# Moving two of four LRU column tiles into the S5 column pass, with twelve token places and a lighter GpSimd

## Chip, cores and metric

One core of a Trainium2 chip runs the whole program. The metric is the device time of one execution in microseconds (us), lower is better.

## What is computed

The reference is one transformer-like layer: a hybrid mixer and then a SwiGLU FFN, both with normalised, modulated input. What matters here is the mixer's front half:

```
h_lat = rms_norm(x, g) * (1 + sc1) + sh1          # 2048 tokens x 1024
h_ctx = rms_norm(ctx, g) * (1 + csc1) + csh1      # 256 tokens
u, xr, gr = split(h @ w_in)                       # 512 S5, 512 LRU, 512 gate columns
y_s5 = s5_scan(u) ...                             # complex diagonal states, both directions
y_lru = rglru(conv(xr)) * gelu(gr_lat)            # gate columns for latent tokens alone
out = concat(y_s5, y_lru) @ w_out
```

All of it is float32. A matrix product is made of three float32r products (high by high, high by low, low by high).

## The kernel before

**The work.** The tokens go through in five groups: n = 0 is the 256 context tokens, n = 1 to 4 are 512 latent tokens each. The 1536 columns of `w_in` are twelve column tiles of 128: four S5 tiles, four LRU tiles, four gate tiles. One product, of one group and one column tile, is 8 x 3 matmuls into a PSUM tile `pu`. The context group needs no gate columns.

**Stages.** `front` (line 159) runs three generators beside each other. `vectors` makes the modulation. `s5_prep` makes the S5 parameters and, through `s5_tables`, sixteen rotation tables (`tb`, stored in TAB), the matrices PKE and PKC and, last, MD from `kx`. `u_pass` makes the four S5 tiles of all five groups: for each group it loads the tokens (`xt`), scales them by their norm (line 352), and `turn` transposes them (`pt`), modulates (`y`), splits them into high and low (`ht`), and stores `y` in HD for groups 0 to 3. Two sets of eight `ht` tiles serve alternate groups, so the next group's turning may begin while the current group's products still run. Its results go to UD.

`mix` (line 183) then runs `s5_main`: 16 channel pairs in two directions, 32 states. A state is four small products `pv` on PE, then some ten instructions on VectorE (lines 753 to 770) with two scans, and the outputs `py` are products again. As filling work between them, `rest_pass` (line 807) makes the LRU and gate tiles: group 4 first, whose `ht` tiles are still in place, then groups 0 to 3, whose tokens come back from HD (`hty`) and are split again (`ht<-hty`). It has fourteen places for these. `AHEAD` says how many of its 36 products are written ahead of the first state, and `S5_FILL` how much filling a state is owed.

**The order.** Inside `s5_main` the PE order is the written one. Everywhere else a scheduler at build time sets each engine's order, and every engine then works through its instructions in that order.

**A table's steps** (`s5_tables`, lines 697 to 709): on GpSimd two scalings of a ramp (`tbf`), a rounding in two steps (`tbw`) and a subtraction; on VectorE two corrections (line 702); on ScalarE sines; on VectorE a product (line 707); on ScalarE the last two steps.

Of the kernel before, what the change touches and what calls it, by code (L numbers as in the profile page):

```python
# [9 lines left out]
F32 = mybir.dt.float32  # L10
# [35 lines left out]
class Hybrid:  # L46
# [102 lines left out]

    AHEAD = 8  # L150
    S5_FILL, CONV_FILL, DECAY_FILL, GATES_FILL = 4.2, 0.1, 2.0, (0, 2, 2, 2)
    VW = 5
# [5 lines left out]
    def front(self):  # L158

        self.ies, self.ues = ExitStack(), ExitStack()  # L160
        self.wip = self.pool(self.ies, "winp", 1)

        self.htp = self.pool(self.ies, "htp", 1)
# [138 lines left out]
    def load_w_in(self, col0, pool, stage, place=None):  # L302

        ws = []
        src = self.A["w_in"][0].rearrange("(k p) f -> p k f", p=128)
        for m in range(4):
            c0 = col0 + m * 128
            if place:
                wh, wl = (t.rearrange("p a (b f) -> p (a b) f", f=128) for t in place[m])
            else:  # L310
                wh, wl = (pool.tile([128, KT, 128], F32R, name=f"win{nm}{m}") for nm in "hl")
            raw = stage()
            self.nc.sync.dma_start(raw, src[:, :, c0:c0 + 128])
            self.split(wh, wl, raw)
            ws.append((wh, wl))
        return ws

    def ht(self, n, k):
        return self.htp.tile([128, 2, 512], F32R, name=f"ht{n % 2}_{k}")

    def u_pass(self, es):

        nc, A = self.nc, self.A
        sp = self.pool(es, "us", 2)
        lent = iter(range(KT))
        whole = lambda: self.ht(1, next(lent)).bitcast(F32).rearrange("p a f -> p (a f)")

        def load(n):
            if n == 0:
                xt = [whole() for _ in range(2)]  # L330
# [13 lines left out]
        def norm(tiles, junk):  # L344
# [29 lines left out]
        def product(n, m, hts, after):  # L374
# [7 lines left out]
            ut = sp.tile([128, 512], F32, name="ut")  # L382
            if n == 0:
                uv = ut[:, :CTX].rearrange("p (t j) -> p t j", t=T)
# [8 lines left out]

        ws0 = [whole().rearrange("p (k f) -> p k f", k=KT) for _ in range(4)]
        xs = load(0)
        norm(xs, whole())
        yield
        ws = self.load_w_in(0, self.wip, ws0.pop)
        yield
# [4 lines left out]
        hts = []  # L404
        turn(0, xs, hts, range(KT))
        raw = lambda: xp.tile([128, D], F32, name="xt").rearrange("p (k f) -> p k f", k=KT)
        for n in range(5):
# [10 lines left out]
            for m in range(4):  # L418
                if (n, m) == (4, 2):

                    place = [(self.ht(1, i), self.ht(1, i + 4)) for i in range(4)]
                    self.wrest = self.load_w_in(512, None, raw, place=place)
                product(n, m, hts, after)
                yield 5.2
# [261 lines left out]
    def s5_tables(self, p, st, fh, fl):  # L686
# [6 lines left out]
        for k in range(NPAIR):  # L693
            f = st.tile([128, 2, NPOS], F32, name="tbf")
            w = st.tile([128, 2, NPOS], F32, name="tbw")
            for d in range(2):
                nc.gpsimd.tensor_scalar(f[:, d], jr, fh[:, d * 16 + k:d * 16 + k + 1], 0.0, op0=MUL, op1=ADD)
            nc.gpsimd.tensor_scalar(w, f, 1.0, MAGIC, op0=MUL, op1=ADD)
            nc.gpsimd.tensor_scalar(w, w, 1.0, -MAGIC, op0=MUL, op1=ADD)
            nc.gpsimd.tensor_tensor(f, f, w, op=SUB)  # L700
            for d in range(2):
                v.scalar_tensor_tensor(f[:, d], jr, fl[:, d * 16 + k:d * 16 + k + 1], f[:, d], op0=MUL, op1=ADD)
            tb = st.tile([128, 2, 2, NPOS], F32, name="tb")
# [104 lines left out]
    def rest_pass(self, es):  # L808

        nc = self.nc  # L810
        st = self.pool(es, "ist", 2)
        hp = self.pool(es, "gtp", 1)
# [15 lines left out]
        for n, after in ((4, 0), (0, 1), (1, 2), (2, 3), (3, None)):  # L828
# [6 lines left out]

            for m in range(8 if n else 4):
                more(min(MORE, m + 1 if n else 2 * m + 2))
                pu = ps.tile([128, 512], F32, name="pu")
                wh, wl = self.wrest[m]
# [3 lines left out]
                ut = st.tile([128, 512], F32, name="iev")  # L843
                if m >= 4:
                    nc.scalar.activation(ut, pu, AF.Gelu_apprx_tanh)
                    nc.sync.dma_start(self.GGD[m - 4][:, (n - 1) * 512:n * 512], ut)
                elif n == 0:
                    nc.scalar.activation(ut[:, :CTX].rearrange("p (j t) -> p t j", t=T),
                                         pu[:, :CTX].rearrange("p (t j) -> p t j", t=T), AF.Copy)
                    nc.sync.dma_start(self.XRD[m][:, 0:CTX], ut[:, :CTX])  # L850
                else:

                    for t in range(2):
                        nc.scalar.activation(ut.rearrange("p (c t r) -> p t r c", c=8, t=2)[:, t],
                                             pu.rearrange("p (t r c) -> p t r c", t=2, c=8)[:, t], AF.Copy)
                    dst = self.XRD[m][:, CTX:CTX + SEQ].rearrange("p (c x) -> p c x", c=8)
                    nc.sync.dma_start(dst[:, :, (n - 1) * 64:n * 64], ut.rearrange("p (c x) -> p c x", c=8))
                yield 5.4 if n else 2.8
# [721 lines left out]
```

## Time and profile before

| | |
|---|---|
| Median of 3 runs | 2353.78 us (2349.54 to 2354.25) |
| The profiled execution: own time | 2348.0 us |
| Its span, first to last instruction | 2346.2 us |
| Busy: PE, VectorE, ScalarE, GpSimd | 2105.7, 1714.1, 966.3, 905.5 us |
| Mean granted TensorE clock | 0.947 |

The span is what the profile's rows cover; 1.8 us of the execution's own time lie around it. PE is busy for 90% of the span, but as an average over stages: the first 240 us and the stage of the states differ much from the FFN behind them, so the stages are read apart. In the rows DVE is VectorE, ACT is ScalarE, POOL is GpSimd, SP is the engine that issues most DMAs, PEclk the granted share of full clock.

### The profile page before, as it was taken

What the parts mean: (1) busy time and instruction counts of PE and PEld (TensorE: products, weight loads), DVE (VectorE), ACT (ScalarE), POOL (GpSimd) and SP (SyncE); (2) the same over time, 40 slices, a digit from 0 to 9 for tenths busy, and PEclk for the clock granted to TensorE, in tenths of its full rate; (3) what the DMA queues carried; (4) which work ended last, traced back from release to release, by engine and by line L of the source; (5) the groups of instructions that cost most, each with busy time, mean ns of one, the idle gap of its engine ahead of it and who ended that gap; (6) DMA issues with size and microseconds to landing.
All of it is one profiled execution on the core that took longest, in us unless ns stands there. A gap on an engine that the chain in (4) does not pass through costs nothing. (4 is left out here: it accounts for less than half of the span.)

```text
span 2346.2 us, 27426 instructions
## 1 busy us (share of the span) xinstructions
PE 2105.7 (90%) x9460; PEld 1664.3 (71%) x9460; DVE 1714.1 (73%) x2227; ACT 966.3 (41%) x1511; POOL 905.5 (39%) x560
## 2 busy tenths in 40 slices
PE   6578999899475699869999999999999999999997
PEld 1466776667374578747888888788888878888885
DVE  6987338997898766866778887987777763534669
ACT  2566421211766734773333333433333333232433
POOL 4786240340000002342334553666665620400674
PEclk8689999999788899979999999999999999999999
DMA  8476866664334366883444333544444374734673
GB/s 246 154 219 232 257 208 180 208 195 128 118 110 145 109 202 211 273 259 122 135 143 135 108 99 127 171 161 148 152 152 155 137 255 158 229 105 143 205 268 115
DMA packets 311626, 403.28 MB, mean 172 GB/s; under 512 B 60176, under 2 KB 222528, under 8 KB 309952
## 3 DMA queue, kind: packets, MB, share of 16 engines
q1 hardware_dynamic: 311360, 401.50, 52.8%
q8 instruction: 75, 1.23, 0.2%
q14 instruction: 63, 0.52, 0.1%
q0 software_dynamic: 128, 0.04, 0.0%
HBM read 269.33 MB, written 132.12 MB: 171 GB/s over the span
## 5 line engine op out<-in xcount | busy, mean ns | idle before, releaser
L70 PE MATMUL fp<-op,fws 128*128 128x512 f32 x1232 | 485.0, 394 | 7.8 <-ACT op L59 7.1
L71 PE MATMUL fp<-op,fws 128*128 128x512 f32 x1232 | 485.1, 394 | 5.3 <-DVE op L62 3.1
L72 PE MATMUL fp<-op,fws 128*128 128x512 f32 x1232 | 484.0, 393 | 0.0
L70 PEld LDWEIGHTS fp<-op,fws 128*128 128x128 f32 x1232 | 232.6, 189 | 62.1 <-ACT op L59 9.2
L71 PEld LDWEIGHTS fp<-op,fws 128*128 128x128 f32 x1232 | 232.2, 188 | 60.5 <-DVE op L62 5.4
L72 PEld LDWEIGHTS fp<-op,fws 128*128 128x128 f32 x1232 | 232.2, 189 | 51.5
L1337 POOL TENSOR_TENSOR fs<-fraw 128x512 f32<-128x512 f32 x44 | 65.8, 1495 | 490.8 <-DMA fraw<-in_w_ffn_in_dram 408.4
L1017 PE MATMUL po<-gw,ga 128*128 128x512 f32 x616 | 240.7, 392 | 4.3 <-ACT ga L59 2.9
L1018 PE MATMUL po<-gw,ga 128*128 128x512 f32 x616 | 240.5, 392 | 0.9 <-DVE gw L62 0.9
L1019 PE MATMUL po<-gw,ga 128*128 128x512 f32 x616 | 237.8, 391 | 2.4 <-DVE ga L62 2.4
L62 DVE TENSOR_TENSOR fws<-fraw,fws 128x512 fp32r<-128x512 f32 x132 | 128.8, 977 | 58.2 <-ACT fws L59 57.3
L59 ACT ACTIVATE fws<-fraw 128x512 fp32r<-128x512 f32 x132 | 82.8, 629 | 142.6 <-PE fp L72 76.0
L1017 PEld LDWEIGHTS po<-gw,ga 128*128 128x128 f32 x616 | 116.6, 189 | 29.7 <-ACT ga L59 3.8
L1019 PEld LDWEIGHTS po<-gw,ga 128*128 128x128 f32 x616 | 116.0, 188 | 27.8 <-DVE ga L62 3.9
L1018 PEld LDWEIGHTS po<-gw,ga 128*128 128x128 f32 x616 | 116.5, 189 | 26.2 <-DVE gw L62 1.7
L62 DVE TENSOR_TENSOR ga<-gys,ga 128x1024 fp32r<-128x1024 f32 (+2 forms) x88 | 119.2, 1358 | 13.3 <-ACT ga L59 13.0
L71 PE MATMUL pu<-ht,winh 128*128 128x512 f32 (+1 forms) x288 | 115.1, 400 | 14.5 <-DVE ht L62 14.5
L62 DVE TENSOR_TENSOR fws<-fs,fws 128x512 fp32r<-128x512 f32 x132 | 118.2, 896 | 9.7 <-ACT fws L59 8.0
L59 ACT ACTIVATE fws<-fs 128x512 fp32r<-128x512 f32 x132 | 82.4, 625 | 94.3 <-PE fp L72 92.5
L70 PE MATMUL pu<-ht,winh 128*128 128x512 f32 (+1 forms) x288 | 114.2, 405 | 3.7 <-ACT ut L390 3.2
L72 PE MATMUL pu<-ht,winl 128*128 128x512 f32 (+1 forms) x288 | 113.2, 393 | 0.0
L62 DVE TENSOR_TENSOR gw<-graw,gw 128x512 fp32r<-128x512 f32 x44 | 37.8, 860 | 84.0 <-ACT gw L59 83.9
(509 smaller groups left out, 4733.8 us busy)
## 6 DMA issues: line engine op xcount, KB each, us to landing
fraw<-in_w_ffn_in_dram SPq DMA_DIRECT2D x88, 512.0 KB, 4.4
graw<-in_w_ffn_out_dram SPq DMA_DIRECT2D x99, 256.0 KB, 3.9
gys<-S SPq DMA_DIRECT2D x44, 512.0 KB, 3.8
A<-faf SPq DMA_DIRECT2D x33, 512.0 KB, 2.6
S<-ost SPq DMA_DIRECT2D x33, 512.0 KB, 3.1
alw<-in_w_ada_dram SPq DMA_DIRECT2D x24, 512.0 KB, 5.1
ost<-A SPq DMA_DIRECT2D x22, 512.0 KB, 4.3
gys<-A SPq DMA_DIRECT2D x22, 512.0 KB, 5.1
```

Of the source, the lines that this page charges most:

```text
L59: self.nc.scalar.activation(hi, src, AF.Identity)
L62: (eng or self.nc.vector).tensor_tensor(lo, src, hi.bitcast(F32), op=SUB)
L70: mm(ps, wh, xh, start=first, stop=False)
L71: mm(ps, wh, xl, start=False, stop=False)
L72: mm(ps, wl, xh, start=False, stop=last)
L1017: mm(ps, xh, wh, start=first, stop=False)
L1018: mm(ps, xh, wl, start=False, stop=False)
L1019: mm(ps, xl, wh, start=False, stop=last)
L1337: g.tensor_tensor(s[0], a21, a22, op=ADD)
```

## The change

It does four things.

- `u_pass` makes six column tiles for each group: the four S5 tiles and LRU tiles 0 and 1 (`end_rest` stores these). The weights of the two are kept in four new tiles `wx`. `rest_pass` makes the other two LRU tiles and the four gate tiles: 26 products instead of 36. `AHEAD` goes from 8 to 2, `S5_FILL` from 4.2 to 3.9.
- The `ht` tiles are one ring of twelve places instead of two sets of eight. Tiles 4 to 7 of the next group take the places of tiles 0 to 3 of the current one, so they are turned within the last product (steps 40 to 43 of 48), tiles 0 to 3 at steps 22 to 34. `rest_pass` has twelve places instead of fourteen: four `wx` and the eight of group 4.
- A table's two ramp scalings go from GpSimd to ScalarE; the second half of the rounding and the subtraction become one VectorE instruction of 128x576.
- The scaling of the tokens goes from GpSimd to ScalarE.

```diff
-    AHEAD = 8
-    S5_FILL, CONV_FILL, DECAY_FILL, GATES_FILL = 4.2, 0.1, 2.0, (0, 2, 2, 2)
+    AHEAD = 2
+    S5_FILL, CONV_FILL, DECAY_FILL, GATES_FILL = 3.9, 0.1, 2.0, (0, 2, 2, 2)
...
-    def ht(self, n, k):
-        return self.htp.tile([128, 2, 512], F32R, name=f"ht{n % 2}_{k}")
+    HT = 12
+
+    def ht(self, i):
+        return self.htp.tile([128, 2, 512], F32R, name=f"ht{i % self.HT}")
+
+    def wx(self, i):
+        return self.wxp.tile([128, 2, 512], F32R, name=f"wx{i}")
...
-                nc.gpsimd.tensor_scalar(x, x, rs[:, i:i + 1], 0.0, op0=MUL, op1=ADD)
+                nc.scalar.activation(x, x, AF.Copy, scale=rs[:, i:i + 1])
...
-                ht = self.ht(n, k)
+                ht = self.ht(8 * n + k)
...
+            if m >= 4:
+                self.end_rest(n, m - 4, pu, ut)
...
+        ws += self.load_w_in(512, None, lambda: next(stages), [(self.wx(2 * i), self.wx(2 * i + 1)) for i in range(2)])
...
-                if nxt and i % 2 and len(nh) < KT and i >= 13:
+                if nxt and i in (22, 26, 30, 34, 40, 41, 42, 43):
                     turn(n + 1, nxt, nh, (len(nh),))
...
-            for m in range(4):
+            for m in range(6):
...
-                nc.gpsimd.tensor_scalar(f[:, d], jr, fh[:, d * 16 + k:d * 16 + k + 1], 0.0, op0=MUL, op1=ADD)
+                nc.scalar.activation(f[:, d], jr, AF.Copy, scale=fh[:, d * 16 + k:d * 16 + k + 1])
             nc.gpsimd.tensor_scalar(w, f, 1.0, MAGIC, op0=MUL, op1=ADD)
-            nc.gpsimd.tensor_scalar(w, w, 1.0, -MAGIC, op0=MUL, op1=ADD)
-            nc.gpsimd.tensor_tensor(f, f, w, op=SUB)
+            v.scalar_tensor_tensor(f, w, -MAGIC, f, op0=ADD, op1=SUB)
...
-        MORE = 6
-        places = cycle([lambda i=i: hp.tile([128, 2, 512], F32R, name=f"ht{i}") for i in range(MORE)] +
-                       [lambda k=k: self.ht(0, k) for k in range(KT)])
+        MORE = 4
+        places = cycle([lambda i=i: self.wx(i) for i in range(MORE)] + [lambda i=i: self.ht(i) for i in range(32, 40)])
...
-            for m in range(8 if n else 4):
+            for i in range(6 if n else 2):
```

**The instruction order at the first state, on PE.** Before, the last eight products ahead of the first `pv` are all of `rest_pass`, for group 4 (gate weights `winh`, `winl`); behind it stand context products of 256 columns (operands `ht`, weights in `ht` places):

```order
L70 MATMUL pu<-ht_7_2174,winh_2494 128x512
L71 MATMUL pu<-ht_7_2174,winh_2494 128x512
L72 MATMUL pu<-ht_7_2174,winl_2495 128x512
L747 MATMUL pv<-u,pe 64x288 x4
L70 MATMUL pu<-ht_2517,ht_0_2369 128x256
L71 MATMUL pu<-ht_2517,ht_0_2369 128x256
L72 MATMUL pu<-ht_2517,ht_4_2370 128x256
```

With the change the first row of `pv` stands two products ahead of the end of `u_pass` (its last S5 product ahead of it, weights `winh`, then its two LRU products, weights `wx`):

```order
L70 MATMUL pu<-ht_2548,winh_475 128x512
L71 MATMUL pu<-ht_2548,winh_475 128x512
L72 MATMUL pu<-ht_2548,winl_476 128x512
L774 MATMUL pv<-u,pe 64x288
L70 MATMUL pu<-ht_2402,wx_565 128x512
L71 MATMUL pu<-ht_2402,wx_565 128x512
L72 MATMUL pu<-ht_2402,wx_566 128x512
```

The first state's last `pv` rows stand behind 720 `pu` matmuls (30 products, six of the context) instead of 672 (28, four of the context), the second state's behind 792 instead of 720. The last product of `s5_prep` (`pk`) stands behind 456 `pu` matmuls instead of 336. In both orders the last `pv` row has 1320 to 1344 of all 1344 `pu` matmuls ahead of it.

**On VectorE at the same place.** Before, splits of tokens read back (`hty`) stand ahead of the first state and inside it:

```order
L62 TENSOR_TENSOR ht_2_2860<-hty,ht_2_2860 128x512
L62 TENSOR_TENSOR ht_3_2865<-hty,ht_3_2865 128x512
L62 TENSOR_TENSOR ht_4_2898<-hty,ht_4_2898 128x512
L753 TENSOR_TENSOR ta<-pv,tab 128x576
L754 TENSOR_TENSOR tb__2812<-pv,tab 128x576
L62 TENSOR_TENSOR ht_5_2903<-hty,ht_5_2903 128x512
L62 TENSOR_TENSOR ht_6_2961<-hty,ht_6_2961 128x512
L62 TENSOR_TENSOR ht_7_2966<-hty,ht_7_2966 128x512
L755 TENSOR_TENSOR ta<-ta,tb__2812 128x288
```

With the change weight splits (`winl`) stand ahead of it and the first token splits behind its last row:

```order
L62 TENSOR_TENSOR winl_2764<-xt,winh_2763 128x1024
L62 TENSOR_TENSOR winl_2770<-xt,winh_2769 128x1024
L780 TENSOR_TENSOR ta<-pv,tab 128x576
L781 TENSOR_TENSOR tb__2894<-pv,tab 128x576
L782 TENSOR_TENSOR ta<-ta,tb__2894 128x288
L783 TENSOR_TENSOR ta<-ta,tb__2894 128x288
L786 SCALAR_TENSOR_TENSOR zz<-rho,ta 128x288 x2
L793 TENSOR_TENSOR xa<-zz,tab 128x512
L794 TENSOR_TENSOR xb<-zz,tab 128x512
L796 TENSOR_TENSOR sf_2904<-xa,xb 128x256
L797 TENSOR_TENSOR sf_2904<-xa,xb 128x256
L62 TENSOR_TENSOR wx_2789<-hty,wx_2789 128x256
```

Of the 32 token splits eleven stood ahead of the first state; now none does.

**On GpSimd, at the first tables of `s5_prep`** (`tbf` and `tbw` are a table's tiles, `s5pow` the powers for PKE and PKC), before:

```order
L697 TENSOR_SCALAR tbf<-jramp,s5fh 128x288 x2
L698 TENSOR_SCALAR tbw<-tbf 128x576
L699 TENSOR_SCALAR tbw<-tbw 128x576
L700 TENSOR_TENSOR tbf<-tbf,tbw 128x576
L627 TENSOR_TENSOR s5pow_920<-s5w_418,s5w_419 128x512
```

and with the change:

```order
L726 TENSOR_SCALAR tbw<-tbf 128x576 x4
L655 TENSOR_TENSOR s5pow_880<-s5w_417,s5w_418 128x512
L660 TENSOR_TENSOR s5pow_880<-s5w_419,s5w_420 128x512
L655 TENSOR_TENSOR s5pow_974<-s5w_417,s5w_418 128x576
L726 TENSOR_SCALAR tbw<-tbf 128x576 x2
```

Of a table's five GpSimd instructions one is left, and the powers stand close behind each other.

## Rows read from the trace of the kernel before

**Rows 1.** Busy time by stage: us, busy us of each engine (xinstructions), PEclk, DMA share, GB/s.

```profile
77.00:235.00 158.00, 117.61 (x588) 91.11 (x587) 132.65 (x180) 100.09 (x169) 120.52 (x91) 0.85 0.66 214
235.00:334.00 99.00, 92.57 (x429) 74.75 (x428) 25.30 (x38) 37.85 (x61) 40.48 (x24) 0.98 0.79 236
334.00:585.00 251.00, 240.81 (x1248) 173.89 (x1250) 224.93 (x368) 44.65 (x92) 49.94 (x30) 0.96 0.62 178
```

**Rows 2.** Whom PE waited for from 82 to 334 us: us in total, times, longest.

```profile
PE pu L71 <- DVE ht L62: 14.5, 8, 3.2
PE pp L647 <- POOL s5pow L627: 7.7, 4, 3.1
PE pk L667 <- POOL s5pow L627: 4.6, 3, 2.6
PE pt L360 <- DVE y L367: 3.8, 3, 1.4
PE pu L70 <- ACT ut L390: 3.2, 3, 1.9
```

**Rows 3.** Busy time of PE alone beside the rest, 300 to 325 us.

```profile
300.00:325.00 25.00, 25.00 (x112) 20.62 (x110) 2.23 (x4) 6.29 (x10) 20.16 (x12) 1.00 0.64 186
```

**Rows 4.** Groups by line, 0 to 520 us: busy us, mean ns | idle before.

```profile
L667 PE MATMUL pk<-s5pow,s5lhs 128*32 128x128 f32 x128 | 24.0, 350 | 12.5 <-POOL s5pow L627 10.9 <-DVE s5pow L634 1.5
...
L360 PE MATMUL pt<-ident,xt 128*128 128x128 f32 x128 | 19.3, 277 | 7.1 <-POOL xt L352 2.9 <-DVE y L367 2.4 <-ACT y L365 1.6
...
L647 PE MATMUL pp<-ident,s5pow 128*128 128x128 f32 x64 | 13.3, 345 | 14.7 <-POOL s5pow L627 12.4 <-POOL s5pow L632 2.3
```

**Rows 5.** PE in order of time, context products: start, us.

```profile
120.80 0.28 PE L72 MATMUL pu<-ht,winl 128*128 128x256 f32 x1
...
123.20 0.28 PE L71 MATMUL pu<-ht,winh 128*128 128x256 f32 x1
```

**Rows 6.** Tile pt: ns min/median/max, first and last start.

```profile
L360 PE MATMUL pt<-ident,ht x16: 318/421/477, 76.6 to 98.0; 128*128 128x128 f32 x16
```

**Rows 7.** Tile pv, the states' first products and first readers.

```profile
L747 PE MATMUL pv<-u,pe x256: 406/406/687, 325.2 to 573.8; 128*64 128x288 f32 x128
L753 DVE TENSOR_TENSOR ta<-pv,tab x32: 743/750/758, 334.2 to 574.3; 128x576 f32<-128x576 f32 x32
```

**Rows 8.** VectorE in order of time at the first state.

```profile
333.59 0.69 DVE L62 TENSOR_TENSOR ht<-hty,ht 128x512 fp32r<-128x512 f32 x1 [9.62 <-ACT ht L59]
334.20 0.75 DVE L753 TENSOR_TENSOR ta<-pv,tab 128x576 f32<-128x576 f32 x1
...
335.53 1.88 DVE L62 TENSOR_TENSOR ht<-hty,ht 128x512 fp32r<-128x512 f32 x3
...
341.51 0.75 DVE L753 TENSOR_TENSOR ta<-pv,tab 128x576 f32<-128x576 f32 x1
```

**Rows 9.** Groups on GpSimd, 0 to 235 us.

```profile
L697 POOL TENSOR_SCALAR tbf<-jramp,s5fh 128x288 f32<-128x288 f32 x32 | 35.3, 1113 | 14.9 <-DVE tb L707 11.4 <-DVE exqm L447 3.5
L700 POOL TENSOR_TENSOR tbf<-tbf,tbw 128x576 f32<-128x576 f32 x16 | 29.7, 1862 | 0.5
...
L352 POOL TENSOR_SCALAR xt<-xt,rs 128x1024 f32<-128x1024 f32 x12 | 20.5, 1731 | 3.0 <-DVE rs L94 3.0
L699 POOL TENSOR_SCALAR tbw<-tbw 128x576 f32<-128x576 f32 x16 | 14.3, 899 | 0.4
```

**Rows 10.** Tile tbf, the table steps on VectorE: ns min/median/max.

```profile
L702 DVE SCALAR_TENSOR_TENSOR tbf<-jramp,s5fl,tbf x32: 498/513/1678, 38.4 to 222.9; 128x288 f32<-128x288 f32 x32
...
L707 DVE SCALAR_TENSOR_TENSOR tb<-tbw,tbf x16: 735/754/1850, 44.2 to 225.7; 128x576 f32<-128x576 f32 x16
```

**Rows 11.** The same two groups by line, 0 to 520 us.

```profile
L702 DVE SCALAR_TENSOR_TENSOR tbf<-jramp,s5fl,tbf 128x288 f32<-128x288 f32 x32 | 24.1, 793 | 5.1 <-POOL tbf L700 5.1
...
L707 DVE SCALAR_TENSOR_TENSOR tb<-tbw,tbf 128x576 f32<-128x576 f32 x16 | 15.4, 961 | 5.5 <-ACT tbf L706 5.5
```

**Rows 12.** ScalarE on a token tile, 0 to 335 us.

```profile
L76 ACT ACTIVATE junk<-xt 128x1024 bf16<-128x1024 f32 x16 | 16.8, 1049 | 3.3 <-DMA xt<-in_x_dram 3.3
```

More of the change, by code (lines that the diff above doesn't have):

```diff
@@ L161, in front @@
         self.wip = self.pool(self.ies, "winp", 1)
+        self.wxp = self.pool(self.ies, "winx", 1)
         self.htp = self.pool(self.ies, "htp", 1)
@@ L305, in load_w_in @@
         src = self.A["w_in"][0].rearrange("(k p) f -> p k f", p=128)
-        for m in range(4):
+        for m in range(len(place or range(4))):
             c0 = col0 + m * 128
@@ L316, in load_w_in, with end_rest @@
         return ws
-    def ht(self, n, k):
-        return self.htp.tile([128, 2, 512], F32R, name=f"ht{n % 2}_{k}")
+    HT = 12
[3 more added lines that the diff above has]
+        return self.wxp.tile([128, 2, 512], F32R, name=f"wx{i}")
+    def end_rest(self, n, m, pu, ut):
+        nc = self.nc
+        if m >= 4:
+            nc.scalar.activation(ut, pu, AF.Gelu_apprx_tanh)
+            nc.sync.dma_start(self.GGD[m - 4][:, (n - 1) * 512:n * 512], ut)
+        elif n == 0:
+            nc.scalar.activation(ut[:, :CTX].rearrange("p (j t) -> p t j", t=T),
+                                 pu[:, :CTX].rearrange("p (t j) -> p t j", t=T), AF.Copy)
+            nc.sync.dma_start(self.XRD[m][:, 0:CTX], ut[:, :CTX])
+        else:
+            for t in range(2):
+                nc.scalar.activation(ut.rearrange("p (c t r) -> p t r c", c=8, t=2)[:, t],
+                                     pu.rearrange("p (t r c) -> p t r c", t=2, c=8)[:, t], AF.Copy)
+            dst = self.XRD[m][:, CTX:CTX + SEQ].rearrange("p (c x) -> p c x", c=8)
+            nc.sync.dma_start(dst[:, :, (n - 1) * 64:n * 64], ut.rearrange("p (c x) -> p c x", c=8))
     def u_pass(self, es):
@@ L324, in u_pass @@
         sp = self.pool(es, "us", 2)
-        lent = iter(range(KT))
-        whole = lambda: self.ht(1, next(lent)).bitcast(F32).rearrange("p a f -> p (a f)")
+        whole = lambda i: self.ht(i).bitcast(F32).rearrange("p a f -> p (a f)")
         def load(n):
             if n == 0:
-                xt = [whole() for _ in range(2)]
+                xt = [whole(8 + i) for i in range(2)]
                 src = A["ctx"][0].rearrange("(j t) d -> t j d", t=T)
@@ L382, in product @@
             ut = sp.tile([128, 512], F32, name="ut")
-            if n == 0:
+            if m >= 4:
+                self.end_rest(n, m - 4, pu, ut)
+            elif n == 0:
                 uv = ut[:, :CTX].rearrange("p (t j) -> p t j", t=T)
@@ L392, in product @@
                 nc.sync.dma_start(self.UD[m][:, s0:s0 + 2, NC_:NPOS], uv)
-        ws0 = [whole().rearrange("p (k f) -> p k f", k=KT) for _ in range(4)]
+        stages = (whole(i).rearrange("p (k f) -> p k f", k=KT) for i in (4, 5, 6, 7, 10, 11))
         xs = load(0)
-        norm(xs, whole())
+        norm(xs, whole(10))
         yield
-        ws = self.load_w_in(0, self.wip, ws0.pop)
+        ws = self.load_w_in(0, self.wip, lambda: next(stages))
         yield
@@ L414, in after @@
             def after(i):
-                if nxt and i % 2 and len(nh) < KT and i >= 13:
+                if nxt and i in (22, 26, 30, 34, 40, 41, 42, 43):
                     turn(n + 1, nxt, nh, (len(nh),))
-            for m in range(4):
+            for m in range(6):
                 if (n, m) == (4, 2):
-                    place = [(self.ht(1, i), self.ht(1, i + 4)) for i in range(4)]
-                    self.wrest = self.load_w_in(512, None, raw, place=place)
+                    place = [(self.ht(40 + 2 * i), self.ht(41 + 2 * i)) for i in range(2)]
+                    self.wrest = self.load_w_in(768, None, raw, place)
                 product(n, m, hts, after)
@@ L696, in s5_tables @@
             for d in range(2):
-                nc.gpsimd.tensor_scalar(f[:, d], jr, fh[:, d * 16 + k:d * 16 + k + 1], 0.0, op0=MUL, op1=ADD)
+                nc.scalar.activation(f[:, d], jr, AF.Copy, scale=fh[:, d * 16 + k:d * 16 + k + 1])
             nc.gpsimd.tensor_scalar(w, f, 1.0, MAGIC, op0=MUL, op1=ADD)
-            nc.gpsimd.tensor_scalar(w, w, 1.0, -MAGIC, op0=MUL, op1=ADD)
-            nc.gpsimd.tensor_tensor(f, f, w, op=SUB)
+            v.scalar_tensor_tensor(f, w, -MAGIC, f, op0=ADD, op1=SUB)
             for d in range(2):
-                v.scalar_tensor_tensor(f[:, d], jr, fl[:, d * 16 + k:d * 16 + k + 1], f[:, d], op0=MUL, op1=ADD)
+                v.scalar_tensor_tensor(f[:, d], jr, fl[:, d * 16 + k:d * 16 + k + 1], f[:, d], op0=MUL, op1=SUB)
             tb = st.tile([128, 2, 2, NPOS], F32, name="tb")
@@ L834, in more @@
                     nxt.extend(fetch(after, k) for k in range(len(nxt), upto))
-            for m in range(8 if n else 4):
-                more(min(MORE, m + 1 if n else 2 * m + 2))
+            for i in range(6 if n else 2):
+                more(min(MORE, i + 1 if n else 2 * i + 2))
                 pu = ps.tile([128, 512], F32, name="pu")
-                wh, wl = self.wrest[m]
+                wh, wl = self.wrest[i]
                 for k in range(KT):
@@ L842, in rest_pass @@
                              k == 0, k == KT - 1)
[L843 to L857, printed above, removed]
+                self.end_rest(n, i + 2, pu, st.tile([128, 512], F32, name="iev"))
                 yield 5.4 if n else 2.8
```

1 line of the change is left out of this document (removed).

## The prediction

> **What bounds the kernel now.** I read three stages ahead of the FFN in the table of busy times by stage, then whom PE waited for in the first two, then the order at the first state. Up to 235 us [rows 1] no engine is full: VectorE is busy for 132.65 of 158 us, GpSimd for 120.52, PE for 117.61 at a granted clock of 0.85. Here `u_pass` and `s5_prep` feed each other. From 235 to 334 PE is busy for 92.57 of 99 us and VectorE for 25.30: column products alone. From 334 to 585, the states, PE is busy for 240.81 of 251 us and VectorE for 224.93: both nearly full. So PE bounds the second and third stage, and its idle time lies in the first.
>
> PE's waits there are for VectorE's splits (14.5 and 3.8 us), for GpSimd's powers (7.7 and 4.6) and for ScalarE's evictions (3.2) [rows 2], 33.8 us in these five lines.
>
> **PE's work up to the first state, before.** A 512-column matmul takes 25.00/112 = 0.223 us [rows 3], so a full product of 24 takes 5.36 us; twenty steps of 256 columns took 2.40 us [rows 5], so a context product takes 2.9. Ahead of the first `pv` stand 24 full and 4 context products: 128.6 + 11.5 us. To them come 144 transposes at 19.3/128 [rows 4], 21.7 us, and of `pk` (24.0) and `pp` (13.3) the seven eighths that stand behind the first transposes, 32.6. Together 194.4 us. They ran from 76.6 [rows 6] to 325.2 us [rows 7], 248.6 us: **54 us of slack**, idle or at the lower clock.
>
> VectorE took up the first state at 334.2, not at 325.2: a split that waited 9.62 us for a token tile stood ahead of it in its queue [rows 8].
>
> **The change, part by part.**
>
> *Two column tiles move to the front.* The sum of column products is the same before and after. `u_pass` gets 8 full and 2 context products more, 48.7 us; the eight products ahead of the first state lose their place there. By the order, the first state now stands behind 24 full and 6 context products: 128.6 + 17.3 + 21.7 + 32.6 = 200.2 us.
>
> *The start of that stretch.* Six of the new VectorE instructions and two weight splits come ahead of the first `y`. A 576-wide one took 735 to 1850 ns [rows 10], and I take 0.75 us; three 512-wide splits took 1.88 [rows 8], so a 1024-wide one some 1.25. That is 4.5 + 2.5 = 7 us later, less some 2 for a lighter GpSimd: start at 81.6. With slack s the first state starts at 81.6 + 200.2 + 1 + s = 282.8 + s, the last 1 us being its own `pv`. Nothing stands ahead of it on VectorE that waits for a read-back. Before it was 334.2: equal at s = 51.4.
>
> *What becomes of the slack.* The products fill holes in which PE waited for `s5_prep`, the more so as GpSimd loses four of five table steps and the token scaling: 35.3 + 29.7 + 14.3 + 20.5 us [rows 9], 100 us in all, most of them beside the 120.52 that it was busy in the first stage [rows 1]. I take the waits for GpSimd's powers (12.3) down to 2, those for VectorE (18.3) down to 12, and of the other 23 us half gone, as denser work also meets a higher clock: 2 + 12 + 12, and 5 for the tighter ring, so **s = 31**. The ends are 12 (all five waits of rows 2 and another 8 us gone) and 60 (below).
>
> *VectorE's own account in the front.* It gains 16 instructions at 0.74 to 0.96 us [rows 10, 11], 12 to 15 us. It loses delays: line 702 took 24.1 us for 32, at its median of 513 ns it would be 16.4; line 707 took 15.4, at 754 ns 12.1 [rows 10, 11]; both ran beside GpSimd. That is 11 us in two groups; the splits of `u_pass` have such outliers too. I take the two as even, so `s5_prep` ends about as now.
>
> The long ones among these are explained by a rule of the Trainium skill ("SBUF — State Buffer", Who interferes with whom): a VectorE instruction with two SBUF inputs and a GpSimd one that reads SBUF exclude each other for a whole instruction. The rows' maxima of 1678 and 1850 ns against medians of 513 and 754 agree. By the rule the new instruction, which has two such inputs, pays too when a power is under way.
>
> *ScalarE* gets 32 scalings of 288 and 18 of 1024. The latter cost 1.05 us [rows 12]; the former between 0.30 (288/1024 of it) and 1.05, I take 0.5: 35 us in all, beside 100.09 busy of 158 [rows 1]. It stays under 90%, off the path, but its queue gets longer; that is in the 12 us of s. Against this move speaks a rule of the skill ("ScalarE: Activation LUTs", Rules for kernel authors) that gives multiplications to VectorE; here VectorE is the fuller one [rows 1], and the row on line 76 against GpSimd's 1731 ns a tile [rows 9] says ScalarE is no slower.
>
> *SP and GpSimd queues.* The stores of the two tiles move with them to the front, two more weight loads also; their number stays. GpSimd's queue holds nothing behind the removed steps but powers.
>
> *The states.* What PE has left from the first state on stays the same within 3 us: 624 matmuls, 48 of them short, against some 640 with 96 short. But all 32 token splits now lie inside, where eleven had run ahead of it or in it: +3 us. The second state stands three full products behind the first, 16 us, where a state took 7.3 [rows 8]; VectorE idles there, and catches up, as PE is the bound. At each change of group the next tiles 4 to 7 wait for the last product's first steps, 33 matmuls or 7.4 us ahead of need, behind a state on VectorE: +3 us in all. So +6.
>
> *Sum.* 31 - 51.4 + 6 = -14 us against the profiled execution's 2348.0, that is 2334. The median of the runs shown, 2353.78, lies 5.8 above the profiled one, so **2340**. Later stages are left as they are: the page's chain of waits names FFN products there and no edit reaches them.
>
> **Rivals.** Each moves s or the last term.
>
> *A, slower: the holes don't fill.* PE works in order, so an added product fills a hole only if it stands there and its tokens are ready. In front of each new group four tiles can be turned only within the last product. A tile costs VectorE 0.63 for its split [rows 8] and half a `y`, with transposes and ScalarE's high part some 3 us for the first and 1.3 for each more: 6.8 us, with 24 matmuls, 5.4 us, to cover it. Four changes leave 6 us bare, and more behind `s5_prep`'s instructions on VectorE: s = 54 + 6 = 60, +15 us, **2368**. It decides from s = 45 on. For it: VectorE, PE's largest wait, gets no lighter. Against it: 12.3 us of waits for GpSimd.
>
> *B, no change: the states take it back.* The start comes 20 us sooner, but VectorE pays eleven splits (7 us), the hole behind the first state (16 - 7.3 = 9) and four changes of group with 1 us each, all on top of its 224.93: about 20 back, **2354**. For it: VectorE is at 90% there. Against it: PE at 96%, so VectorE has slack of its own.
>
> *C, faster: the clash of VectorE and GpSimd was the bound.* Lines 702 and 707 fall by 11 us, the splits likewise, `s5_prep` ends sooner, and the waits of rows 2 go: s = 12, -33 us, **2320**. For it: the maxima of rows 10. Against it: the new instructions give 12 to 15 us back. The rule of the skill cited above would have it so, if powers alone clash too seldom to matter.
>
> That the change doesn't do what it says can be left out: the order shows it on PE, VectorE and GpSimd.
>
> **How the numbers follow.** The forecast has 0.52, with a range of its own of 2328 to 2349 (s from 19 to 40); C 0.22, B 0.11, A 0.15. The range of 8 in 10 reaches from 2316, into C, to 2361, half way into A. A measurement tells about 0.2%, 4.7 us, from no change. Faster by more: the forecast but for 0.03 at its upper edge, and C, 0.71. Within it: B and that edge, 0.14. Slower: A, 0.15.
>
> **What would show it.** The first state's reader on VectorE at about 314 us instead of 334.2; PE's busy share from 77 to 235 us up from 117.61 of 158 to 135 or more; waits of `pp` and `pk` for GpSimd under 4 us; lines 702's and 707's means near their medians; the last state's end about 14 us sooner, and a stretch of states of about 257 us instead of 251. The prediction is wrong if the wait of column products for VectorE's splits grows past 30 us, or if the stretch of states grows by 15 us or more.

## The result, and the profile after

The changed kernel took **2326.36 us** (median of 4 runs, 2322.2 to 2331.62) against 2351.66 for the kernel before (4 runs): ratio 0.9896, 95% interval 0.9874 to 0.9919, some 25 us or 1.0% faster. 14 us had been forecast. The sign is right and the time lies inside the wide range of 2316 to 2361, but below the forecast's own 2328 to 2349; and the runs below show that the gain came from another part of the change than the one that the forecast built on.

The profiled executions, 2348.0 and 2329.66 us, differ by 18.3 only. From the two traces, start of some events in us:

| | before | after | sooner by |
|---|---|---|---|
| last column kernel of `s5_prep` (`s5kx`, VectorE) | 242.0 | 233.2 | 8.8 |
| last token transpose (`pt`, PE) | 259.1 | 262.6 | -3.5 |
| first state on VectorE (`ta`) | 334.2 | 299.3 | 34.9 |
| second | 341.5 | 323.4 | 18.1 |
| last product of the states (`py`, PE) | 585.3 | 565.6 | 19.7 |
| first product of the LRU's gates (`pg`, PE) | 604.8 | 578.9 | 25.9 |
| first FFN product (`fp`, PE) | 1011.1 | 982.8 | 28.3 |
| end of the span | 2346.2 | 2327.9 | 18.3 |

So 35 us are won at the first state, 17 given back between the first state and the second, 2 won in the rest of the states, 9 more up to the FFN, and 10 lost in the last stage of the profiled execution, where PE stood still once (the view of PE's waits from 1870 us on; line, whom it waited for: us in total, times, longest):

```profile
PE po L1029 <- DVE gw L62: 9.4, 1, 9.4
```

Before, PE's waits for this tile came to 0.9 us. No edit reaches that stage; the section on the unexpected comes back to it. Without these 8.5 us the pair of traces would be 27 us apart, near the 25 of the medians.

Busy time by stage after, the same stretches and columns as [rows 1]:

```profile
77.00:235.00 158.00, 138.24 (x747) 111.54 (x746) 124.39 (x196) 127.99 (x219) 48.13 (x31) 0.92 0.73 235
235.00:334.00 99.00, 94.93 (x424) 75.20 (x423) 42.39 (x54) 32.55 (x50) 38.87 (x20) 0.97 0.68 201
334.00:585.00 251.00, 217.23 (x1131) 154.02 (x1130) 230.13 (x373) 50.73 (x102) 51.30 (x35) 0.92 0.65 194
```

In the first stage GpSimd fell from 120.52 to 48.13 us. VectorE issues 16 instructions more there (196 against 180) and is busy for *less*: 124.39 against 132.65. PE is up from 117.61 to 138.24, at a granted clock of 0.92 instead of 0.85.

The third stretch can't be held against the one before, as the states now end at 565.6 us and 20 us of the LRU's start lie in it. Cut at the states themselves, from the first to the second and from there to their end, before and then after:

```profile
334.20:341.50 7.30, 7.30 (x46) 6.53 (x47) 7.23 (x14) 2.58 (x5) 0.00 (x0) 0.77 0.83 265
341.50:587.20 245.70, 234.09 (x1208) 167.51 (x1207) 217.50 (x355) 41.88 (x86) 49.94 (x30) 0.97 0.62 178
```

```profile
299.30:323.40 24.10, 20.81 (x81) 15.97 (x82) 10.15 (x14) 4.26 (x10) 9.28 (x6) 0.86 0.57 164
323.40:567.00 243.60, 220.95 (x1148) 156.05 (x1148) 222.54 (x365) 45.37 (x93) 50.52 (x30) 0.94 0.64 192
```

Behind the second state PE was at 95% and VectorE at 89%; now both are at 91%. That part is about as long as before (245.7 and 243.6 us). What grew is the hole ahead of it, 24.1 us instead of 7.3, in which VectorE is busy for 10.15.

PE's waits from 76 to 300 us after, to be held against [rows 2]:

```profile
PE pu L71 <- DVE ht L62: 10.9, 4, 3.4
PE pu L70 <- ACT ut L416: 3.4, 2, 2.2
PE pt L384 <- DVE y L391: 2.1, 1, 2.1
PE pt L384 <- ACT y L389: 1.5, 1, 1.5
PE pp L675 <- POOL s5pow L660: 1.3, 2, 0.7
```

The waits for GpSimd's powers went from 12.3 us (7.7 and 4.6) to 1.3, the others from 21.5 to 17.9. The steps of a table, by tile, as in [rows 10]:

```profile
L725 ACT ACTIVATE tbf<-jramp,s5fh x32: 517/522/535, 27.1 to 190.2; 128x288 f32<-128x288 f32 x32
L729 DVE SCALAR_TENSOR_TENSOR tbf<-jramp,s5fl,tbf x32: 496/514/1573, 31.3 to 199.1; 128x288 f32<-128x288 f32 x32
L726 POOL TENSOR_SCALAR tbw<-tbf x16: 664/678/2646, 28.1 to 192.4; 128x576 f32<-128x576 f32 x16
L727 DVE SCALAR_TENSOR_TENSOR tbf<-tbw,tbf x16: 737/747/1953, 29.8 to 193.1; 128x576 f32<-128x576 f32 x16
...
L734 DVE SCALAR_TENSOR_TENSOR tb<-tbw,tbf x16: 734/753/1164, 40.8 to 204.3; 128x576 f32<-128x576 f32 x16
```

ScalarE's scalings are short and even (517 to 535 ns). VectorE's and GpSimd's still have maxima of one and a half to four times their medians.

And VectorE at the first states, in order of time; [rows 8] has the same place before:

```profile
299.33 0.76 DVE L780 TENSOR_TENSOR ta<-pv,tab 128x576 f32<-128x576 f32 x1 [10.84 <-PE pv L774]
...
312.78 0.42 DVE L62 TENSOR_TENSOR wx<-hty,wx 128x256 fp32r<-128x256 f32 x1 [4.72 <-ACT wx L59]
...
323.41 0.76 DVE L780 TENSOR_TENSOR ta<-pv,tab 128x576 f32<-128x576 f32 x1 [8.39 <-PE pv L774]
```

The first state no longer stands behind a split; but the second comes 24.1 us after it (7.3 before), and VectorE idles for more than half of that.

### The profile page after: what moved, and what is told of

Same layout as the page of the kernel before. It is cut to its first block, busy times and chain, and to the rows that moved or that the text cites. A ratio compares the mean times of both kernels' runs of the same rounds, so it can differ in the third digit from the quotient of the medians.

```text
span 2327.9 us, 27391 instructions
## 1 busy us (share of the span) xinstructions
PE 2101.6 (90%) x9460; PEld 1662.1 (71%) x9460; DVE 1714.1 (74%) x2243; ACT 994.3 (43%) x1561; POOL 808.7 (35%) x478
## 5 line engine op out<-in xcount | busy, mean ns | idle before, releaser
L62 DVE TENSOR_TENSOR ga<-gys,ga 128x1024 fp32r<-128x1024 f32 (+2 forms) x88 | 113.8, 1299 | 10.8 <-ACT ga L59 10.8
L71 PE MATMUL pu<-ht,winh 128*128 128x512 f32 (+1 forms) x256 | 100.8, 394 | 10.9 <-DVE ht L62 10.9
L70 PE MATMUL pu<-ht,winh 128*128 128x512 f32 (+1 forms) x256 | 102.3, 404 | 6.7 <-ACT ut L416 3.4
L62 DVE TENSOR_TENSOR gw<-gch,gw 128x512 fp32r<-128x512 f32 x44 | 51.6, 1172 | 71.5 <-ACT gw L59 71.5
```

The source lines that it names most:

```text
L62: (eng or self.nc.vector).tensor_tensor(lo, src, hi.bitcast(F32), op=SUB)
L70: mm(ps, wh, xh, start=first, stop=False)
L71: mm(ps, wh, xl, start=False, stop=False)
```

## The experiments

Theories at the start: **the holes** (the forecast: column products fill PE's idle time in the front; VectorE's own account is even) and **the clash** (rival C: GpSimd's reads hold VectorE up, and GpSimd's relief is the gain). Each kernel was timed beside the kernel before on the same chip; ratios are to it, and where kernels of different chips are compared, the ratios decide. No edit fixes the order that the scheduler sets at build time, so every kernel below also has an order of its own; where that matters it is said.

**Which half gains.** Two kernels with one half of the change each. The engine moves are the diff's hunks on the token scaling and on `s5_tables`; the first kernel is the changed one without them, the second the kernel before with them:

```diff
-                nc.gpsimd.tensor_scalar(x, x, rs[:, i:i + 1], 0.0, op0=MUL, op1=ADD)
+                nc.scalar.activation(x, x, AF.Copy, scale=rs[:, i:i + 1])
...
-                nc.gpsimd.tensor_scalar(f[:, d], jr, fh[:, d * 16 + k:d * 16 + k + 1], 0.0, op0=MUL, op1=ADD)
+                nc.scalar.activation(f[:, d], jr, AF.Copy, scale=fh[:, d * 16 + k:d * 16 + k + 1])
...
-            nc.gpsimd.tensor_scalar(w, w, 1.0, -MAGIC, op0=MUL, op1=ADD)
-            nc.gpsimd.tensor_tensor(f, f, w, op=SUB)
+            v.scalar_tensor_tensor(f, w, -MAGIC, f, op0=ADD, op1=SUB)
```

(The difference now has the opposite sign, so the correction behind it, line 702 before, subtracts it instead of adding it.)

Columns and places alone (these three pieces undone in the changed kernel):

> The change with the table steps and the token scaling left on GpSimd as before: only the two column tiles, the twelve places and the constants. Holes theory (the added products fill PE's idle time in the front by themselves): 2326 to 2335, first state at 300 to 308 us. Clash theory (GpSimd's relief is what counts): 2346 to 2360, first state at 325 us or later, GpSimd busy about 120 of 158 us from 77 to 235. Both needed: 2336 to 2346.

Measured: 2350.1 us, ratio 0.9989 (0.9974 to 1.0005): no change that can be told. The time is the clash theory's; the first state, at 316.7 us, lies between the two theories. The second state comes at 341.3 us, where it came before (341.5).

Engine moves alone (these three pieces in the kernel before):

> The kernel before with the table steps and the token scaling moved as the change does, columns and places as before. Holes theory: within 5 us of the kernel before (2347 to 2355), since PE's work from 235 to 334 us stays as it is and the first state stands behind the same products. Clash theory: 2326 to 2338, the preparation (last kx) at 225 us or sooner and the first state at 315 us or sooner. Both needed: 2340 to 2347.

Measured: 2327.4 us, 0.9889 (0.9871 to 0.9907): a gain as large as that of the whole change. Part of it could be the order: here the first state stands behind 480 `pu` matmuls on PE and comes at 271.2 us, as the eight products of `AHEAD` now lie between it and the second. The second state stands behind 720 as before, and comes at 321.7. Two more kernels put back one part of the engine moves each in the changed kernel, the token scaling (the first pair of lines) and the tables (the rest):

> The change with the token scaling alone back on GpSimd (five groups, some 25 us of GpSimd in 18 instructions). If the token scaling matters: 5 us or more slower than the change (2331 and up). If only the tables matter or neither: within 4 us of the change's 2326.

> The change with the table steps alone back on GpSimd (80 us of GpSimd back, 12 to 15 us of VectorE and some 17 us of ScalarE saved). Clash theory: 10 us or more slower than the change (2336 and up). Holes theory: within 5 us of the change's 2326.

Measured: token scaling back 2331.85 us, 0.9914 (0.9893 to 0.9936), which the intervals don't separate from the changed kernel; tables back 2343.16 us, 0.996 (0.9946 to 0.9973), so the table steps carry most of it. In these two the counts of column products ahead of the first and second state are the changed kernel's.

These four say which part, but not why: the steps went from GpSimd, and to another engine, and the powers behind them on GpSimd's queue moved up. **Reads, or the queue?** Two kernels keep all that the change does and give GpSimd its old load back as work without a reader, once with reads and once without:

```diff
+            for d in range(2):
+                nc.gpsimd.tensor_scalar(w[:, d], jr, fh[:, d * 16 + k:d * 16 + k + 1], 0.0, op0=MUL, op1=ADD)
+            nc.gpsimd.tensor_scalar(w, w, 1.0, -MAGIC, op0=MUL, op1=ADD)
+            nc.gpsimd.tensor_tensor(w, w, w, op=SUB)
             nc.gpsimd.tensor_scalar(w, f, 1.0, MAGIC, op0=MUL, op1=ADD)
```

```diff
+            for i in range(9):
+                nc.gpsimd.memset(w, 0.0)
             nc.gpsimd.tensor_scalar(w, f, 1.0, MAGIC, op0=MUL, op1=ADD)
```

> The changed kernel, with GpSimd's removed work put back as work that nobody needs: ahead of the table step that stays on GpSimd, two scalings of 288, one 576-wide scaling and one 576-wide difference are written into the same tile and then overwritten. All that the change computes on ScalarE and VectorE stays there, so only GpSimd's queue is fuller. Theory 1 (clash: VectorE is held up while GpSimd reads SBUF): VectorE's two-input steps of the tables go back up, the last kx comes some 12 to 17 us later than the 233.2 of the changed kernel, and the time is near 2340 (2335 to 2346), as when the tables were put back whole (2343.16). Theory 2 (queue: the powers stand behind the table steps on GpSimd, and the column products' neighbours behind the powers): also near 2340, but the loss then shows as waits of PE for powers, and it is the same in echo_write. Theory 3 (the chain of a table got shorter, or ScalarE is the better engine for it): 2326 to 2330.

> The same place and the same tile, but nine memsets of 576, which read nothing: at the 525 ns that a 512-wide memset took in the kernel before, 5.3 us a table, where the four removed steps took 5.0. Theory 1 (clash with GpSimd's reads): no loss, 2326 to 2330, VectorE's steps at their short times. Theory 2 (queue): as echo_read, near 2340. A third possibility, that GpSimd's writes alone hold VectorE up, gives a loss as large as that of echo_read with VectorE's steps stretched.

Measured, side by side: with reads **2349.21 us, ratio 1.0 (0.9983 to 1.0017)**, the whole gain gone; with memsets **2326.12 us, 0.9904 (0.9889 to 0.992)**, nothing lost. The first stage, reads and then memsets:

```profile
77.00:235.00 158.00, 128.42 (x687) 102.68 (x687) 130.15 (x191) 119.97 (x207) 103.53 (x81) 0.89 0.65 207
```

```profile
77.00:235.00 158.00, 138.75 (x755) 111.99 (x756) 124.92 (x197) 129.08 (x223) 107.10 (x140) 0.93 0.74 234
```

GpSimd is as full in the one (103.53 us) as in the other (107.10). With reads VectorE is busy for longer with fewer instructions, PE issues 687 matmuls instead of 755, and the last `s5kx` comes at 246.6 us instead of 232.9. The second state comes at 340.5 us with reads and at 323.7 with memsets. PE's waits for powers are 11.9 us with reads and 7.0 with memsets, against 1.3 in the changed kernel: the fuller queue does delay the powers, but with memsets that cost nothing. So neither the queue alone nor the place where the steps went makes the loss; it comes with GpSimd's reading. One thing is not held fixed: both orders have 720 `pu` matmuls ahead of the first state and 456 ahead of the last `pk`, but the last `pp` stands behind 336 of them with reads and 432 with memsets (432 in the changed kernel), so a part of the loss may be the order's.

How long VectorE is held up can be summed from the traces: of every VectorE instruction that starts from 30 to 260 us, what it took above the shortest of the same tiles and shape in any of the profiles.

| kernel | held up, us | second state, us | ratio |
|---|---|---|---|
| before | 54.8 | 341.5 | 1 |
| columns and places alone | 55.0 | 341.3 | 0.9989 |
| changed, with GpSimd's added reads | 46.9 | 340.5 | 1.0 |
| changed, tables back | 47.3 | 338.1 | 0.996 |
| changed, half the tables back (below) | 44.9 | 331.0 | 0.9951 |
| changed, token scaling back | 38.4 | 327.4 | 0.9914 |
| changed, with memsets | 34.0 | 323.7 | 0.9904 |
| changed | 31.7 | 323.4 | 0.9896 |
| changed, powers on VectorE (below) | 11.2 | 317.9 | 0.9886 |

But for the added reads, the second state and the time follow the hold-up, down to some 32 us of it; below that little more is won.

GpSimd's own steps show the other side of it (groups by line, 50 to 260 us: busy us, mean ns), with reads and with memsets:

```profile
L655 POOL TENSOR_TENSOR s5pow<-s5w,s5w 128x512 f32<-128x512 f32 (+1 forms) x16 | 32.9, 2058 | 26.6 <-PE pp L675 11.9 <-DVE s5w L654 10.1 <-issue 4.2
L727 POOL TENSOR_SCALAR tbw<-jramp,s5fh 128x288 f32<-128x288 f32 x28 | 28.0, 1008 | 46.7 <-ACT tb L740 41.9 <-DMA MD<-s5kx 4.7
```

```profile
L727 POOL MEMSET tbw<- 128x576 f32 x114 | 65.7, 581 | 29.0 <-ACT tb L738 24.4
```

A reading scaling of 288 took 1008 ns in the mean, a writing memset of twice the width 581. The Trainium skill's rule that the prediction weighed ("SBUF — State Buffer", Who interferes with whom) also says that a GpSimd instruction which only writes does not contend with a two-input one of VectorE; this pair of runs agrees.

**Half the tables, both ways.** The last two GpSimd steps alone: put back in the changed kernel, and moved alone in the kernel before (the third piece of the diff above, ScalarE and columns untouched).

> The changed kernel with the second half of the table steps alone back on GpSimd: the 576-wide subtraction of the constant and the 576-wide difference (0.9 and 1.8 us), in place of one VectorE instruction of 0.75 us; the two 288-wide scalings stay on ScalarE. Theory 1 (the loss follows the time in which GpSimd reads): 2.7 of the 5.0 us a table come back, so about half of what putting all four back cost (17 us), 8 to 10 us: 2334 to 2337. Theory 2 (the price is in the scalings, whose VectorE partner is the longest stretched): 2327 to 2330. Theory 3 (the price is in these two, of which the difference has two inputs): 2340 to 2344.

Measured: 2339.36 us, 0.9951 (0.9935 to 0.9967). That lies between theories 1 and 3. Beside 0.996 for all four steps put back, nearly all of the loss comes with these two, more than their share of the reading time; the intervals overlap, so the proportion stays open.

> The kernel before with one edit: the last two table steps of GpSimd (0.9 and 1.9 us) become one VectorE instruction of 0.75 us. ScalarE gets nothing, no column moves. Theory 1 (clash): VectorE's list in the front grows by some 14 x 0.75 = 10 us, but GpSimd's reads fall by 14 x 2.76 = 39 us of 120, and VectorE's 45 us of stretch by about a third; net gain 5 to 12 us, 2340 to 2347. Theory 2 (VectorE's amount of work decides, and the prediction's account was even): 2349 to 2357. Theory 3 (the relief came from ScalarE's part): slower, 2358 to 2365.

Measured: 2344.54 us, 0.9969 (0.9952 to 0.9987), by the ratio some 7 us faster, although the edit only moves work from GpSimd to VectorE. Its first stage:

```profile
77.00:235.00 158.00, 123.54 (x620) 96.35 (x621) 130.17 (x197) 106.04 (x179) 87.82 (x62) 0.85 0.68 222
```

VectorE: 197 instructions in 130.17 us, where it had 180 in 132.65, and the hold-up is 40.4 us instead of 54.8. This is the step that the prediction took as even, by itself; but here too the eight products of `AHEAD` moved behind the first state (480 `pu` matmuls ahead of it), so the 7 us are not the step's alone.

**The rest of GpSimd's reads.** The powers' sums and differences to VectorE as well:

```diff
-                    nc.gpsimd.tensor_tensor(flat(out[:, 0]), flat(x0), flat(x1), op=SUB)
+                    v.tensor_tensor(flat(out[:, 0]), flat(x0), flat(x1), op=SUB)
...
-                        nc.gpsimd.tensor_tensor(flat(out[:, 1]), flat(x0), flat(x1), op=ADD)
+                        v.tensor_tensor(flat(out[:, 1]), flat(x0), flat(x1), op=ADD)
```

> The changed kernel with the 24 sums and differences of the powers (lines 655 and 660, 512- and 576-wide, 1.6 to 1.9 us each) on VectorE too, at 0.67 to 0.75 us each there: GpSimd reads hardly anything in the front any more. Theory 1 (clash): VectorE's own list grows by 24 x 0.71 = 17 us, but of its 28 us above the shortest time of each form between 50 and 235 us most goes, and each power is ready 1.1 us sooner; the last kx comes 5 us sooner than 233.2 to 3 us later, the time 2318 to 2328. Theory 2 (what counts is VectorE's amount of work, and GpSimd's relief only helped as far as it was moved to ScalarE): the last kx some 12 to 17 us later, 2336 to 2342.

Measured: 2325.64 us, 0.9886 (0.9862 to 0.9911), with this first stage:

```profile
77.00:235.00 158.00, 142.56 (x766) 115.14 (x767) 115.29 (x217) 131.68 (x223) 10.04 (x10) 0.95 0.73 231
```

217 instructions of VectorE in 115.29 us. Most of the clash is gone (11.2 us held up), the first state comes 5 us sooner (294.3), yet the time can't be told from the changed kernel's. PE is at 142.56 of 158 us here, so little may be left to win in this stage; that was not tried by itself.

**Why the states give time back.** The hole behind the first state, and the ring of places:

```diff
-    AHEAD = 2
+    AHEAD = 0
```

> The changed kernel with AHEAD 0 instead of 2: the products that stand between the first and the second state go. In the changed kernel the second state begins 24 us after the first (7 us in the kernel before). Theory 1 (that hole delays VectorE, which bounds the states at 232 of 267 us): second state some 10 us sooner, last state 4 to 8 us sooner than 559.2, about 2320. Theory 2 (VectorE catches up; the states end by waits inside them, or the product that the hole held is missing later): last state within 2 us of 559.2, 2324 to 2329.

Measured: **2317.2 us (2312.37 to 2321.91), 0.9866 (0.9849 to 0.9883)**; on the same chip the memset kernel and the next one took 2326.12 and 2324.45. The states on VectorE, first to last, and PE's wait from 554 to 600 us:

```profile
L780 DVE TENSOR_TENSOR ta<-pv,tab x32: 744/751/758, 297.4 to 537.4; 128x576 f32<-128x576 f32 x32
```

```profile
PE pgl L70 <- ACT gyh L59: 12.8, 1, 12.8
```

First state to last `py` is 256.4 us (297.4 to 553.8) instead of 266.3. The hole to the second state shrank from 24.1 to 13.7 us, and behind it the states took 242.7 us, as in the changed kernel (242.2): VectorE doesn't catch up what it lost in the hole, which had cost 10. Against the changed kernel's 0.9896 (0.9874 to 0.9919) the intervals just overlap; against the memset kernel's 0.9904 (0.9889 to 0.992) they don't. Of the 12 us won at the last `py` (553.8 against 565.6), 6 are left at the LRU's first gate product (572.6 against 578.9); the wait shown is only 1 us longer than the changed kernel's 11.7, so what takes the rest stays open.

```diff
-        MORE = 4
-        places = cycle([lambda i=i: self.wx(i) for i in range(MORE)] + [lambda i=i: self.ht(i) for i in range(32, 40)])
+        MORE = 6
+        hp = self.pool(es, "gtp", 1)
+        places = cycle([lambda i=i: self.wx(i) for i in range(4)] +
+                       [lambda i=i: hp.tile([128, 2, 512], F32R, name=f"gt{i}") for i in range(2)] + [lambda i=i: self.ht(i) for i in range(32, 40)])
```

> The changed kernel with fourteen places for tokens in the second pass instead of twelve, as many as the kernel before had. Theory 1 (the tighter ring costs the states what the forecast missed of their +15 us): the single wait of a product for the high part of a token tile (7.1 us) and VectorE's 11.1 us behind it go, the last state comes 5 to 7 us sooner than 559.2, about 2320. Theory 2 (those waits are hidden behind VectorE's own work): last state within 2 us, 2324 to 2329.

Measured: 2324.45 us, 0.9899 (0.9882 to 0.9915); the last state comes at 561.8, not sooner than 559.2. The tighter ring costs nothing that can be told, nor did both together help:

> The changed kernel with AHEAD 0 and fourteen places together. With AHEAD 0 alone (2317.2) VectorE still waited 12.5 us for high parts of token tiles in the states. Theory 1 (with the hole gone, the tight ring decides): 3 to 6 us better, 2311 to 2314. Theory 2 (VectorE is the bound of the states, its waits for tiles lie where PE is waited for anyway): 2315 to 2319.

Measured: 2326.69 us, 0.9893 (0.9872 to 0.9915), worse than either theory. Its interval overlaps that of AHEAD 0 alone (0.9849 to 0.9883), so a loss is not shown. Of the 14 us between the two profiled executions 8.5 are PE's wait for `gw` in the last stage (9.4 us against 0.9), 4 lie within the states; why those 4, stays open.

**Does the column move matter at all?** AHEAD 0 in the kernel that has the engine moves alone (there from 8):

> The engine moves alone, columns as before, with AHEAD 0 instead of 8. With 8 the second state came 50 us after the first, but PE was busy for 258 of 267 us there. Theory 1 (PE bounds the states when the eight columns' products stay behind; the hole costs nothing): no gain, 2324 to 2331, so the column move is what lets AHEAD 0 gain. Theory 2 (the hole costs here as in the changed kernel, and the column move is worth nothing either way): 2315 to 2321.

Measured: 2337.62 us, 0.9948 (0.9929 to 0.9968), 10 us *slower* than with AHEAD 8, which neither theory had. The states end at 534.7 us, but column products run on to 573.0 and the gates start at 591.1: without the column move those products are left over as a tail. So AHEAD 0 pays only with the column move, and the column move shows a gain only with AHEAD 0: with the AHEAD of 2 that came with it, it adds nothing to the engine moves (0.9896 beside 0.9889). How much the pair adds over the engine moves with AHEAD 8 is not settled, as 0.9866 (0.9849 to 0.9883) and 0.9889 (0.9871 to 0.9907) overlap.

**Both gains together:** AHEAD 0 and the powers on VectorE.

> The changed kernel with AHEAD 0 and the sums and differences of the powers on VectorE. Theory 1 (two gains in two stages, which add): first state at some 293 us, last py some 5 us ahead of the 553.8 of AHEAD 0 alone, ratio to the kernel before 0.984 to 0.986. Theory 2 (the states or the LRU's start have a bound of their own that takes the 5 us back): 0.986 to 0.989.

Measured: 2319.24 us, 0.9872 (0.9851 to 0.9892). First state 293.7, last `py` 552.5: of 4 us at the first state 1 is left behind the states, as theory 2 has it. The lowest ratio is that of the changed kernel with AHEAD 0; the intervals don't separate the two.

## Why the prediction was wrong in size

- **The step that failed: "VectorE's own account in the front".** It set 12 to 15 us of new instructions against 11 us of delays lost and took "the two as even, so `s5_prep` ends about as now". The 16 new ones cost 13.6 us (16 at a mean of 0.852), as forecast. The delays lost were mis-sized. Of the 54.8 us that VectorE was held up before, 31.7 were left, 2 of them in the new instructions, so 25 us went where the account had 11. Lines 702 and 707 gave 6 of the 11 (the mean of line 702's successor, 693 ns, stayed well above its median of 514). The largest part sat in the splits of the token tiles, 10 us (11.1 to 1.1), which the account named ("the splits of `u_pass` have such outliers too") and did not add up; the products for the powers gave 4. The last `s5kx` came at 252.0 us with the columns alone and at 233.2 with the engine moves, 19 us apart, not even.
- **What that did to the sum.** The start of the stretch was put 5 us later, at 81.6; the first transposes came at 76.7 us, as before. With PE's 200.2 us of work from there, 1 for its own `pv` and the first state at 299.3, PE's slack came out at 21, under the 31 taken and inside the ends of 12 and 60. The waits for powers (to 1.3, forecast 2) and for VectorE (13.0, forecast 12) were right; the rest is 7 us where the sum had 17 (half of 23, and 5 for the ring). With the columns alone the first transposes came at 83.1 us and the first state at 316.7, a slack of 32: what the prediction had reckoned for the whole change (81.6, 314 and 31) is what the kernel without the engine moves did.
- **The states took back what the column move gave.** With the columns alone the first state came 17.5 us sooner, but the second no sooner at all, and the last `py`, at 581.9, 3 us sooner. From the second state to the last `py` it took 240 to 247 us in fifteen of the sixteen profiled kernels (261 in the engine moves with AHEAD 0), so the second state, not the first, is where the states begin in earnest. The term "+6" for the states measured +15 (299.3 to 565.6 is 266.3, against 251.1), at which the prediction called itself wrong (15 us or more). The two terms of 3 us for splits and changes of group didn't show: behind the second state it was 2 us shorter. The hole, which the sum put at nothing, cost 17 (24.1 against 7.3). The mistake was "VectorE idles there, and catches up, as PE is the bound": behind the hole VectorE was as full as PE (91% each). Rival B had priced the hole at 9.
- **ScalarE's prices** were right: 0.52 us for 288 columns, taken as 0.5, and 127.99 of 158 us in all, under 90%. The Trainium skill's rule on multiplications ("ScalarE: Activation LUTs", Rules for kernel authors), weighed against this move, would have kept them off ScalarE; here they went there and the kernel gained. No run has them on VectorE, so the rule itself was not tested.
- **Not in the sum:** 6 us between the states' end and the gates' first product (13.3 us instead of 19.5).
- **Rivals.** C's mechanism, at 0.22, is the one that the runs bear out, but its price of 2320 took a slack of 12 us, where 21 was measured, and 6 us for the states, where 15 was. B's holds for the column half, by the hole alone. A's (the products don't fill the holes) is refuted by PE's busy time in the first stage: 138.24 us, and 129.54 with the columns alone, against 117.61.

So two errors partly cancelled: the engine moves, to which the sum gave some 10 us of waits for powers and nothing on VectorE, were worth as much as the whole gain, and the column move, on which the sum was built, was worth none with the AHEAD that came with it. That the time still fell into the wide range is in part luck.

## What to carry to other kernels

Where VectorE and GpSimd run side by side, add up what *every* VectorE instruction takes above the shortest of its own shape, not only the two groups with the worst maxima, before you weigh new work on VectorE against it: here VectorE got 16 instructions more and was busy for less. To tell contention from queueing, give the freed engine its load back in a form without the suspected resource; the memsets against the reads told in one pair of runs what the four part-wise kernels could not. And read a stage's start where its steady pace begins, not at its first instruction: here the first state came 35 us sooner and the second 18, and what followed took as long as before. Where two engines are both near full, a hole for one of them is not caught up.

## What was not expected of the hardware

GpSimd's writes alone did little harm: with 114 memsets of 581 ns GpSimd was as busy as with reads, and VectorE was held up for 34.0 us, against 31.7 without them and 46.9 with reads. Of VectorE's instructions the sixteen 64x128 copies from SBUF to SBUF (`s5lhs`) did get longer, by the median 555 ns against 224 in the changed kernel. The hold-up is mutual and long: in the kernel before a 288-wide scaling on GpSimd took from 500 to 4107 ns, by tile:

```profile
L697 POOL TENSOR_SCALAR tbf<-jramp,s5fh x32: 500/970/4107, 28.0 to 208.8; 128x288 f32<-128x288 f32 x32
```

In the last stage PE's wait for `gw` is either about 1 us or 8.4 to 9.4 us in one piece. Of the 16 profiled kernels ten had the long one, with no order by edit: the changed kernel did, the same with AHEAD 0 did not (0.9). What decides it was not tried. It is a third of the change's gain, and about what separates the 18 us between the two profiles from the 25 between the medians, so a single profile can't rank kernels this close.
